# Two edits to a decoder kernel on one core: the last down stage's sums begin one gate pair later, and the gates' first product reads hi and lo token factors side by side

## The chip, the cores and the metric

The kernel runs as one program on one core of a Trainium2 chip. The metric is the device time of one execution in microseconds (us). The median of the runs shown is compared, 1024.15 us for the kernel before. A profiled execution is a run of its own, a little longer; its span goes from the first to the last instruction of the program.

The engines are named as in the profile: PE is TensorE (matmuls), PEld its weight loads, DVE is VectorE, ACT is ScalarE, POOL is GpSimd, SP is SyncE. SP issues most DMA transfers, POOL issues those that add while they copy.

## What is computed

A trunk of two layers on 512 tokens of width 1024, in float32. Layer 0 mixes tokens with a gated short convolution, layer 1 with sliding-window attention. Behind each stands a gated feed-forward block of inner width 2816, which takes most of the time:

```python
def swiglu(h, w_gate_up, w_down):
    g, u = jnp.split(h @ w_gate_up, 2, axis=-1)
    return (jax.nn.silu(g) * u) @ w_down

for l in range(DEPTH):
    h = h + rmsnorm(mixer(h), post_norm)          # short convolution, then attention
    ff = swiglu(rmsnorm(h, ffn_pre_norm[l]), ffn_w_gate_up[l], ffn_w_down[l])
    h = h + rmsnorm(ff, ffn_post_norm[l])
```

## The kernel before, in words

**Number format.** Each float32 factor is split into a high part (ACT copies it to the format fp32r) and a low part (DVE subtracts the high part from the whole). A product of two split factors is three matmuls: high by high, high by low, low by high. `mm3` (lines 190 to 193) issues them. For weights, `prepare` in `Job` makes the high part `whi` at line 469 and the low part `wlo` at line 470.

**Gates.** The 2816 inner columns are 22 slices of 128. Two are computed plainly (`project_first`); the other 20 are ten pairs, q = 0 to 9 in each layer, so 20 pairs in all. A pair multiplies a 2 by 2 arrangement of weight blocks by a 2 by 2 arrangement of token factors (left and right 256 tokens, upper and lower four of the eight token tiles) in seven products instead of eight. `gate_jobs` runs them in the order 1, 2, 6, 5, 7, 3, 4. Every product has eight steps: two outputs e, four tiles k of the contraction. Products 1, 6, 7 and 4 gather in a chain X of two PSUM banks, product 2 in a bank Y, products 5 and 3 in a bank Z.

The token factors of products 6, 5, 7 and 4 are sums of blocks that `factors` makes. They lie side by side, high part in columns 0 to 511 and low part in columns 512 to 1023 of one wide tile. So in chain X a step of products 6, 7 and 4 needs one matmul of `whi` with 512 columns (high and low of 256 tokens, line 1047) and one of `wlo` with 256 columns (line 1050). The left half of the bank then holds the products with the high part, the right half that of `whi` with the low part, and `take` adds both halves to what was gathered. Product 1 reads token tiles 0 to 3 as they are, whose high and low parts lie in separate tiles, and goes through `mm3`: three matmuls of 256 columns a step, all into the left half.

`take` (from line 998) follows each product: for products 1, 6 and 4 ACT copies the left half of a bank into `st` (line 1024), and, except for product 1, DVE adds the right half (line 1026, which the profile shows under line 1008, the helper that issues the addition). Product 7 has four such additions. Behind product 4 DVE multiplies gate and up parts (line 1029). Then come the sums and splits that the down stage needs (`pair_sums`), spread over the next jobs.

**Down stages.** The inner slices are worked off in five rounds (`ROUNDS`). Rounds 0 to 3 multiply by the down weights in seven products as well (`seven`), each round one pair behind its gates; round 4 closes the layer plainly (`close`, or the tail of the kernel). The order in a layer is: pairs 0, 1, 2, down 0, pairs 3, 4, down 1, pairs 5, 6, down 2, pairs 7, 8, 9, down 3. Down 3 is the last down stage.

**The line of jobs.** `in_line` runs these products as jobs. While job j is on PE, the weights of job j + 3 are split on ACT and DVE (`LINE_LEAD`), with four buffers each for `whi` and `wlo` (`N_W`). The raw weights come by SP's DMA (line 440 in `Raw.fetch`) into seven raw tiles (`N_RAW`): the next fetch is issued when a raw tile has been used up.

**Sums of weights.** The seven products need sums of weight blocks. Where a sum isn't made by DVE from raw tiles (line 457; pairs q = 1, 2, 3, 4, 5 and 7, the list `ADDED`), POOL makes it in HBM by DMA ahead of time. `Sums` has four steps: copies of blocks (four of them), two additions, one addition, one addition. `BEGIN` names the event at which each sum begins: `"0p5": "d03"` begins the sums of down stage 3 of layer 0 behind gate pair 5. Events in a layer are `p0` to `p9` (end of a pair) and `s0` to `s3` (end of a down stage). `sum_on` takes one step of every sum under way at each event, and `issue` (line 538) hands the transfers to POOL a few per job, each behind ACT's split of a coming job.

**Buffers.** Tiles come from pools: `big` has 43 slots of 512 columns (`N_SLOT`), `wides` 14 tiles of 1024 columns (`N_WIDE`). The split token factors are pairs of slots: `split` in `Update` (line 338) for the norms, line 645 for the convolution. So are the rotated queries and keys (`rope_split`, line 1245) and the attention outputs (`out` in `Heads`, line 1390). In attention the order of the work is written out by hand (`ORDER`).

Of the kernel before, what the change touches and what calls it, by code (L numbers as in the profile page):

```python
# [11 lines left out]
F32R = mybir.dt.float32r  # L12
# [6 lines left out]
S = 512  # L19
KT = D // P  # L20
# [7 lines left out]

BEGIN = {
# [4 lines left out]
}  # L34


# [15 lines left out]
    "L": "low", "W": "weigh", "O": "out", "Q": "project", "R": "rotate", "H": "split",  # L52
    "G": "weights", "Z": "project", "z": "out",
}
N_SLOT, N_WIDE, N_RAW, N_W = 43, 14, 7, 4
EARLY = 4
HD = 64
NH = 16
# [14 lines left out]
def yoco_kernel(  # L73
# [42 lines left out]
    def slot(s, dt=F32, w=S):  # L116
        return big.tile([P, w], dt, tag="slot", name=name(s), padded_shape=[P, S])

    def wide(s, dt=F32):
        return wides.tile([P, D], dt, tag="wide", name=name(s))  # L120
# [118 lines left out]
    class Update:  # L239
# [3 lines left out]
        def __init__(self, mix, gain, gpres):  # L243
            self.mix, self.gpres, self.gain = mix, gpres, gain
            self.s, self.v, self.r = (
                small.tile([P, n], F32, tag=tag, name=name(tag))
                for tag, n in (("us", 12), ("uv", 8), ("ur", 8))
            )
            self.x = [[None] * KT for _ in gpres]
            self.xn, self.banks, self.parts = {}, {}, {}  # L250
            self.leaves = False

        def load(self, queue=nc.sync):
# [82 lines left out]
                                        ident)  # L336

        def split(self, n, f, hf):
            if self.x[n][f] is None:
                self.x[n][f] = (slot("xhi", F32R), slot("xlo", F32R))  # L340
            hi, lo = self.x[n][f]
            c = slice(hf * 256, (hf + 1) * 256)
            src = self.banks[f % 4, hf][:, (f // 4) * 256 : (f // 4 + 1) * 256]
            nc.scalar.activation(hi[:, c], src, AF.Copy, scale=g(self.gpres[n], f))
            nc.vector.scalar_tensor_tensor(
                out=lo[:, c], in0=src, scalar=g(self.gpres[n], f), in1=hi[:, c].bitcast(F32),
                op0=ALU.mult, op1=ALU.subtract,
            )
# [15 lines left out]
        def factors(self):  # L364


            x = self.x[0]
            made = {p: [] for p in range(1, 8)}
            for p, k0, c in ((1, 0, 0), (2, 4, 0), (3, 4, 256)):
                made[p] = [[a[:, c : c + 256] for a in x[k0 + k]] for k in range(4)]  # L370
            for j in range(2):
                q11, q21, q12, q22 = (self.parts[i, hf, j] for hf in range(2) for i in range(2))

                nc.vector.tensor_tensor(out=q11, in0=q11, in1=q12, op=ALU.subtract)
                nc.vector.tensor_tensor(out=q12, in0=q22, in1=q12, op=ALU.subtract)
                nc.vector.scalar_tensor_tensor(out=q22, in0=q22, scalar=-1.0, in1=q11,
                                               op0=ALU.mult, op1=ALU.subtract)
                nc.vector.scalar_tensor_tensor(out=q21, in0=q22, scalar=-1.0, in1=q21,
                                               op0=ALU.mult, op1=ALU.subtract)
                for p, q in ((6, q22), (5, q11), (7, q12), (4, q21)):  # L380
                    two = wide("xt", F32R)
                    hi, lo = two[:, :S], two[:, S:]
                    two = two.rearrange("p (i c) -> p i c", i=2)
                    nc.scalar.activation(hi, q, AF.Copy)
                    nc.vector.tensor_tensor(out=lo, in0=q, in1=hi.bitcast(F32),
                                            op=ALU.subtract)
                    made[p] += [[hi[:, c : c + 256], lo[:, c : c + 256], two[:, :, c : c + 256]]
                                for c in (0, 256)]
            return made
# [252 lines left out]
        return product  # L642


    xs = [(slot("xhi", F32R), slot("xlo", F32R)) for _ in range(KT)]
    rows = slot("rrow")
    cols = small.tile([P, 4], F32, tag="cols", name=name("cols"))
    ws = [[wsp.tile([P, D], F32R, tag=tag, name=name(tag)) for tag in ("whi", "wlo")]
# [306 lines left out]
    def ffn(l, before, ahead, gain, gpres, following):  # L955

        xs = before.x[0]
# [18 lines left out]
        def gate_jobs(q, factors, out, to, then):  # L976
# [24 lines left out]
            def take(p):  # L1001
                x, y, z = (banks.get(c) for c in "XYZ")
                st, u, gr = kept
                g0, g1 = (gr.rearrange("p (e h c) -> p e h c", e=2, h=2)[:, :, h]
                          for h in range(2))

                def add(out, a, b):
                    nc.vector.tensor_tensor(out=out, in0=a, in1=b, op=ALU.add)  # L1008

                if p == 2:  # L1010
                    add(g0, tiles(y), tiles(st))
                elif p == 5:
                    nc.scalar.activation(u, z, AF.Copy)
                elif p == 3:
                    add(g1, tiles(z), tiles(st))
                else:
                    for e in range(2):
                        a, b = x[e][:, :256], x[e][:, 256:]
                        ste, ue = (v[:, e * 256 : (e + 1) * 256] for v in (st, u))
                        if p == 7:  # L1020
                            add(ue, a, ue)
                            add(ue, b, ue)
                            continue
                        nc.scalar.activation(ste, a, AF.Copy)  # L1024
                        if p != 1:
                            add(ste, b, ste)
                if p == 4:
                    for g, m in ((g0, st), (g1, u)):
                        nc.vector.scalar_tensor_tensor(out=g, in0=tiles(m), scalar=-1.0, in1=g,
                                                       op0=ALU.mult, op1=ALU.mult)  # L1030

            def run(p):
                def products(job):
                    if not kept:
                        kept.extend([slot("st"), slot("st"), wide("gr")])
                    whi, wlo = split[p] if p in split else job.w
                    c = chain[p]
                    opened = c not in banks
                    if opened:
                        banks[c] = ([bank("gx", pools[c]) for _ in range(2)] if c == "X"  # L1040
                                    else bank("g" + c.lower(), pools[c]))
                    steps = [(e, k, slice(e * S + k * P, e * S + (k + 1) * P))
                             for e in range(2) for k in range(4)]
                    kw = {"skip_group_check": True}
                    if c == "X" and len(factors[p][0]) == 3:
                        for e, k, kk in steps:
                            nc.tensor.matmul(banks[c][e], whi[:, kk], factors[p][k][2],  # L1047
                                             start=opened and k == 0, stop=False, **kw)
                        for e, k, kk in steps:
                            nc.tensor.matmul(banks[c][e][:, :256], wlo[:, kk], factors[p][k][0],  # L1050
                                             start=False, stop=k == 3 and p == 4, **kw)
                    else:
                        for e, k, kk in steps:
                            out = (banks[c][e][:, :256] if c == "X"
                                   else banks[c][:, e * 256 : (e + 1) * 256])
                            mm3(out, whi[:, kk], wlo[:, kk], *factors[p][k][:2],
                                opened and k == 0 and (c == "X" or e == 0),
                                e == 1 and k == 3 and p in (2, 3), **kw)
                    take(p)
                return products  # L1060
# [181 lines left out]
        eng.tensor_tensor(out=a, in0=a, in1=sh, op=ALU.add)  # L1242
        return a

    def rope_split(a, eng):
        hi, lo = slot("rhi", F32R), slot("rlo", F32R)
        nc.scalar.activation(hi, a, AF.Copy)
        eng.tensor_tensor(out=lo, in0=a, in1=hi.bitcast(F32), op=ALU.subtract)
        return hi, lo


    class Queries:
# [16 lines left out]
            self.rot = rope(self.ps, eng)  # L1269

        def split(self, eng=nc.gpsimd):
            self.hi, self.lo = rope_split(self.rot, eng)

    class Heads:

# [111 lines left out]
                    skip_group_check=True)  # L1387

        def out(self):
            hi, lo = slot("ohi", F32R), slot("olo", F32R)  # L1390
            nc.scalar.activation(hi, self.po, AF.Copy)
            nc.vector.tensor_tensor(out=lo, in0=self.po, in1=hi.bitcast(F32), op=ALU.subtract)
            at.append((hi, lo))
# [224 lines left out]
```

## Time and profile before

| what | us |
|---|---|
| median of 3 runs (1024.09 to 1025.18) | 1024.15 |
| the profiled execution | 1026.6 |
| its span | 1024.8 |
| PE busy | 1013.6 |
| DVE busy | 857.8 |
| ACT busy | 580.7 |

How to read it: the profile's busy time of PE is the time in which any matmul is under way. Matmuls overlap and their ends are modelled, so the distance between the starts of two matmuls says what one costs, and the duration does not. In a row of the timeline stand the start and the duration in us, the engine, the line of the code, the operation, what it writes and reads, its shape, and in brackets the idle time of the engine before it with what ended it. A row with x8 is eight instructions merged. The chain of waits starts from the last instruction and goes back at each step to what released it. DMA rows tell the time from issue to landing.

### The profile page before, as it was taken

The numbers are of one execution on the slowest core, as the hardware profiler recorded it, in microseconds if no ns is written. First come the engines' busy times: TensorE is split into PE (matmuls) and PEld (weight loads), VectorE is DVE, ScalarE is ACT, GpSimd is POOL, SyncE is SP. The second block draws the span as 40 slices with busy tenths as digits, with TensorE's granted clock in tenths as the row PEclk, the third lists the DMA queues.
The fourth block names the chain that finished last, engine by engine and source line by source line (L and its number), as shares of the span: only waits on it lengthen the run. The fifth ranks groups of instructions, "written<-read, shape, count | busy, mean of one in ns | idle before, by whom it ended". The sixth has DMA issues, their size and how long they took to land.

```text
span 1024.8 us, 16537 instructions
## 1 busy us (share of the span) xinstructions
PE 1013.6 (99%) x6168; PEld 901.8 (88%) x6168; DVE 857.8 (84%) x1440; ACT 580.7 (57%) x1035; POOL 196.7 (19%) x259
## 2 busy tenths in 40 slices
PE   9999999999999999999999999999999999999997
PEld 8888888999899898898898888889998998989986
DVE  5766768889789988988869998778997898889896
ACT  7222445875655454566476776667666554645641
POOL 0443033112111111000122653232111010100001
PEclk9999999999999999999999999999999999999999
DMA  9897789459979699778504889976899576998742
GB/s 356 287 255 232 187 254 348 140 169 281 344 249 299 195 302 318 256 215 303 182 1 152 199 234 281 246 260 156 262 289 333 169 247 228 299 294 245 242 150 82
DMA packets 66576, 244.52 MB, mean 239 GB/s; under 512 B 7872, under 2 KB 8384, under 8 KB 54720
## 3 DMA queue, kind: packets, MB, share of 16 engines
q1 hardware_dynamic: 51328, 145.98, 38.9%
q0 software_dynamic: 14592, 96.48, 37.2%
q8 instruction: 48, 0.79, 0.3%
q10 hardware_dynamic: 576, 1.02, 0.3%
q14 instruction: 32, 0.26, 0.1%
HBM read 237.15 MB, written 102.76 MB: 332 GB/s over the span
## 4 chain that ended last, share of the span: by engine, by line
PE 80%; DVE 11%; DMA 4%; ACT 2%; issue 2%; POOL 0%; DVEq 0%; ACTq 0%
PE gx L1047 10%; PE gx L1050 5%; DMA raw<-in_w_gb_dram 4%; PE pcub L193 4%; PE pcub L191 4%; PE pcub L192 4%; PE gz L193 3%; PE gz L192 3%; PE gz L191 3%; PE px L191 3%; PE px L192 3%; PE px L193 3%; PE pmix L192 2%; PE pmix L191 2%; PE pmix L193 2%
## 5 line engine op out<-in xcount | busy, mean ns | idle before, releaser
L470 DVE TENSOR_TENSOR wlo<-raw,whi 128x1024 fp32r<-128x1024 f32 x225 | 274.6, 1227 | 65.6 <-ACT whi L469 65.6
L469 ACT ACTIVATE whi<-raw 128x1024 fp32r<-128x1024 f32 x225 | 233.8, 1051 | 108.3 <-DVE raw L457 25.0
L1047 PE MATMUL gx<-xt,whi 128*128 128x512 f32 x480 | 120.4, 393 | 0.7 <-DVE st L1008 0.7
L1047 PEld LDWEIGHTS gx<-xt,whi 128*128 128x128 f32 x480 | 86.3, 189 | 16.6 <-DVE st L1008 1.2
L538 POOL DMA_DIRECT2D hsum<-in_w_gb_dram x96 | 63.4, 747 | 141.4 <-ACT whi L469 82.3
L1024 ACT ACTIVATE st<-gx 128x256 f32<-128x256 f32 x120 | 42.7, 379 | 60.8 <-PE gx L1050 36.4
L538 POOL DMA_DIRECT2D hsum<-hsum x32 | 25.2, 789 | 260.1 <-ACT whi L469 208.2
L1050 PEld LDWEIGHTS gx<-xt,wlo 128*128 128x128 f32 x480 | 65.5, 190 | 4.7
L1050 PE MATMUL gx<-xt,wlo 128*128 128x256 f32 x480 | 66.9, 282 | 0.0
L1008 DVE TENSOR_TENSOR st<-gx,st 128x256 f32<-128x256 f32 x160 | 62.8, 420 | 3.4 <-ACT st L1024 1.6
L192 PE MATMUL pcub<-xhi,whi 128*128 128x512 f32 x168 | 65.4, 389 | 0.0
L191 PE MATMUL pcub<-xlo,whi 128*128 128x512 f32 x168 | 65.4, 389 | 0.0
L193 PE MATMUL pcub<-xhi,wlo 128*128 128x512 f32 x168 | 65.4, 389 | 0.0
L1063 ACT ACTIVATE gr<-gr 128x1024 f32<-128x1024 f32 x20 | 21.3, 1063 | 50.6 <-DVE gr L1008 50.6
L191 PE MATMUL px<-wlo,ahi 128*128 128x512 f32 x120 | 46.8, 390 | 0.1
L192 PE MATMUL px<-whi,ahi 128*128 128x512 f32 x120 | 46.7, 389 | 0.0
L193 PE MATMUL px<-whi,alo 128*128 128x512 f32 x120 | 46.7, 389 | 0.0
L193 PE MATMUL gx<-xhi,wlo 128*128 128x256 f32 x160 | 45.4, 284 | 0.8 <-DVE wlo L470 0.8
L193 PE MATMUL gz<-xhi,wlo 128*128 128x256 f32 x160 | 45.5, 284 | 0.0
L191 PE MATMUL gx<-xlo,whi 128*128 128x256 f32 x160 | 45.4, 283 | 0.0
L191 PE MATMUL gy<-xlo,whi 128*128 128x256 f32 x160 | 45.3, 283 | 0.0
L192 PE MATMUL gy<-xhi,whi 128*128 128x256 f32 x160 | 45.3, 283 | 0.0
(265 smaller groups left out, 3062.8 us busy)
## 6 DMA issues: line engine op xcount, KB each, us to landing
hsum<-in_w_gb_dram POOLq DMA_DIRECT2D x96, 512.0 KB, 7.8
raw<-hsum SPq DMA_DIRECT2D x88, 512.0 KB, 7.9
raw<-in_w_gb_dram SPq DMA_DIRECT2D x60, 512.0 KB, 7.7
hsum<-in_w_dn_dram POOLq DMA_DIRECT2D x36, 512.0 KB, 9.1
raw<-in_w_dn_dram SPq DMA_DIRECT2D x32, 512.0 KB, 6.1
hsum<-hsum POOLq DMA_DIRECT2D x28, 512.0 KB, 6.7
raw<-in_w_in_dram SPq DMA_DIRECT2D x21, 512.0 KB, 8.1
hsum<-in_w_dn_dram POOLq DMA_DIRECT2D x12, 768.0 KB, 12.2
```

Source lines behind the costliest of these rows:

```text
L191: nc.tensor.matmul(out, whi, xlo, start=start, stop=False, **kw)
L192: nc.tensor.matmul(out, whi, xhi, start=False, stop=False, **kw)
L193: nc.tensor.matmul(out, wlo, xhi, start=False, stop=stop, **kw)
L469: self.begun = nc.scalar.activation(hi[:, :n], raw, AF.Copy)
L470: nc.vector.tensor_tensor(out=lo[:, :n], in0=raw, in1=hi[:, :n].bitcast(F32), op=ALU.subtract)
L538: nc.gpsimd.dma_start(dst, src, max_dma_last_dim=4 * 4 * S, **kw))
L1008: nc.vector.tensor_tensor(out=out, in0=a, in1=b, op=ALU.add)
L1024: nc.scalar.activation(ste, a, AF.Copy)
L1047: nc.tensor.matmul(banks[c][e], whi[:, kk], factors[p][k][2], start=opened and k == 0, stop=False, **kw)
L1050: nc.tensor.matmul(banks[c][e][:, :256], wlo[:, kk], factors[p][k][0], start=False, stop=k == 3 and p == 4, **kw)
L1063: nc.scalar.activation(kept[2], kept[2], AF.Silu)
```

## The change

It has three parts.

1. `BEGIN`: the sums of the last down stage of each layer (`d03`, `d13`) begin behind pair 6 instead of pair 5.
2. Token tiles 0 to 3 of the norm ahead of a feed-forward block are split into one wide tile, high and low side by side (`BOTH = 4`), and `factors` hands product 1, whose four tiles these are, the view of both parts. So product 1 takes the wide form in all 20 pairs: eight matmuls of 512 columns with `whi`, then eight of 256 columns with `wlo`, in place of 24 of 256 columns. Products 2, 3 and 5 stay as they are. `take` now adds the right half of the banks for product 1 too, two additions on DVE.
3. The pools change from 43 slots and 14 wide tiles to 35 and 18. Beside the token tiles, the convolution's first four, the rotated queries and the first four attention outputs move from slots to wide tiles.

```diff
-    "0f1": "g05", "0p0": "g06", "0p1": "d02", "0p2": "g07", "0p3": "g08", "0s1": "g09", "0p5": "d03",
+    "0f1": "g05", "0p0": "g06", "0p1": "d02", "0p2": "g07", "0p3": "g08", "0s1": "g09", "0p6": "d03",
...
-    "1f0": "g15", "1f1": "g16", "1p0": "d12", "1p2": "g17", "1p3": "g18", "1s1": "g19", "1p5": "d13",
+    "1f0": "g15", "1f1": "g16", "1p0": "d12", "1p2": "g17", "1p3": "g18", "1s1": "g19", "1p6": "d13",
...
-N_SLOT, N_WIDE, N_RAW, N_W = 43, 14, 7, 4
+N_SLOT, N_WIDE, N_RAW, N_W = 35, 18, 7, 4
+BOTH = 4
...
         def split(self, n, f, hf):
+            if self.x[n][f] is None and n == 0 and f < BOTH:
+                two = wide("xhl", F32R)
+                self.x[n][f] = two[:, :S], two[:, S:]
+                self.both[f] = two.rearrange("p (i c) -> p i c", i=2)
...
             for p, k0, c in ((1, 0, 0), (2, 4, 0), (3, 4, 256)):
-                made[p] = [[a[:, c : c + 256] for a in x[k0 + k]] for k in range(4)]
+                made[p] = [[a[:, c : c + 256] for a in x[k0 + k]]
+                           + [two[:, :, c : c + 256] for two in self.both[k0 + k :][:1] if two]
+                           for k in range(4)]
...
                         nc.scalar.activation(ste, a, AF.Copy)
-                        if p != 1:
-                            add(ste, b, ste)
+                        add(ste, b, ste)
...
-                    if c == "X" and len(factors[p][0]) == 3:
+                    if c == "X":
                         for e, k, kk in steps:
                             nc.tensor.matmul(banks[c][e], whi[:, kk], factors[p][k][2],
                                              start=opened and k == 0, stop=False, **kw)
...
-            out = (banks[c][e][:, :256] if c == "X"
-                   else banks[c][:, e * 256 : (e + 1) * 256])
...
-    def rope_split(a, eng):
-        hi, lo = slot("rhi", F32R), slot("rlo", F32R)
+    def rope_split(a, eng, large=False):
+        hi, lo = halves("rhl", F32R) if large else (slot("rhi", F32R), slot("rlo", F32R))
...
-            hi, lo = slot("ohi", F32R), slot("olo", F32R)
+            if self.t < BOTH:
+                hi, lo = halves("ohl", F32R)
+            else:
+                hi, lo = slot("ohi", F32R), slot("olo", F32R)
```

More of the change, by code (lines that the diff above doesn't have):

```diff
@@ L250, in __init__ @@
             self.xn, self.banks, self.parts = {}, {}, {}
+            self.both = [None] * KT
             self.leaves = False
@@ L642, in seven @@
         return product
-    xs = [(slot("xhi", F32R), slot("xlo", F32R)) for _ in range(KT)]
+    xs = [halves("xhl", F32R) if k < BOTH else (slot("xhi", F32R), slot("xlo", F32R))
+          for k in range(KT)]
     rows = slot("rrow")
@@ L1053, in products @@
                         for e, k, kk in steps:
-                            out = (banks[c][e][:, :256] if c == "X"
-                                   else banks[c][:, e * 256 : (e + 1) * 256])
-                            mm3(out, whi[:, kk], wlo[:, kk], *factors[p][k][:2],
-                                opened and k == 0 and (c == "X" or e == 0),
+                            mm3(banks[c][:, e * 256 : (e + 1) * 256], whi[:, kk], wlo[:, kk],
+                                *factors[p][k][:2], opened and e == k == 0,
                                 e == 1 and k == 3 and p in (2, 3), **kw)
@@ L1271, in split @@
         def split(self, eng=nc.gpsimd):
-            self.hi, self.lo = rope_split(self.rot, eng)
+            self.hi, self.lo = rope_split(self.rot, eng, True)
     class Heads:
```

## The prediction

> **What bounds the kernel now.** I read the page first, then the windows of the stages, then single stretches of the timeline. The profiled execution took 1026.6 us, 1.8 more than its span. Of the rows below, the first two are the page's busy times and its chain of waits; a window's columns are its length, the busy time of PE, PEld, DVE, ACT and POOL, the clock, the DMA share and GB/s.
>
> ```profile
> PE 1013.6 (99%) x6168; PEld 901.8 (88%) x6168; DVE 857.8 (84%) x1440; ACT 580.7 (57%) x1035; POOL 196.7 (19%) x259
> PE 80%; DVE 11%; DMA 4%; ACT 2%; issue 2%; POOL 0%; DVEq 0%; ACTq 0%
> ```
> ```profile
> 391.00:410.00 19.00, 19.00 (x86) 15.77 (x86) 14.68 (x21) 6.73 (x9) 2.36 (x3) 1.00 1.02 322
> 410.00:431.00 21.00, 19.97 (x139) 18.20 (x138) 20.29 (x30) 11.77 (x18) 1.56 (x2) 1.00 0.77 256
> ...
> 500.00:600.00 100.00, 98.75 (x662) 85.94 (x662) 86.24 (x226) 67.98 (x177) 41.03 (x49) 1.00 0.44 123
> 600.00:700.00 100.00, 99.57 (x646) 87.00 (x645) 82.71 (x215) 71.93 (x187) 34.65 (x41) 1.00 0.89 257
> ```
>
> The end is set by the stream of matmuls, at clock 1.00: time is won by a shorter stream or by closing its few holes. A matmul's duration is no price, since matmuls overlap; what counts is the distance between starts. These rows of PE's timeline run from product 4 of one gate pair to product 5 of the next (start, duration).
>
> ```profile
> 221.35 2.00 PE L1047 MATMUL gx<-xt,whi 128*128 128x512 f32 x8
> 223.19 1.11 PE L1050 MATMUL gx<-xt,wlo 128*128 128x256 f32 x8
> 224.15 0.28 PE L191 MATMUL gx<-xlo,whi 128*128 128x256 f32 x1
> 227.03 0.28 PE L191 MATMUL gy<-xlo,whi 128*128 128x256 f32 x1
> 229.91 2.00 PE L1047 MATMUL gx<-xt,whi 128*128 128x512 f32 x8
> 232.70 0.28 PE L191 MATMUL gz<-xt,whi 128*128 128x256 f32 x1
> ```
>
> In product 4 the 8 wide matmuls take 223.19 - 221.35 = 1.84 us (0.230 each) and the 8 narrow ones 224.15 - 223.19 = 0.96 (0.120 each). Product 1, 24 narrow ones, takes 227.03 - 224.15 = 2.88 us. Product 6, already in the wide form, takes 232.70 - 229.91 = 2.79.
>
> The largest hole lies in pair 7 of each layer. The next rows are the first matmul of product 1 of pairs 7, 8 and 9 in layer 0 (with the one that stalls), then of pairs 7 and 8 in layer 1.
>
> ```profile
> 410.35 0.39 PE L191 MATMUL gx<-xlo,whi 128*128 128x256 f32 x1
> 411.61 0.39 PE L193 MATMUL gx<-xhi,wlo 128*128 128x256 f32 x1 [0.76 <-DVE wlo L470]
> 431.91 0.28 PE L191 MATMUL gx<-xlo,whi 128*128 128x256 f32 x1
> 451.81 0.28 PE L191 MATMUL gx<-xlo,whi 128*128 128x256 f32 x1
> ...
> 915.65 0.28 PE L191 MATMUL gx<-xlo,whi 128*128 128x256 f32 x1
> 936.28 0.28 PE L191 MATMUL gx<-xlo,whi 128*128 128x256 f32 x1
> ```
>
> An undisturbed pair takes 451.81 - 431.91 = 19.90 us. Pair 7 takes 21.56 in layer 0 and 20.63 in layer 1, so 1.66 + 0.73 = 2.4 us are lost. The row names wlo as what was late; in the chain of waits stand the weight fetches behind it, 19 and 20 us under way:
>
> ```profile
> 389.06 20.07 DMA raw<-in_w_gb_dram
> 896.80 19.04 DMA raw<-in_w_gb_dram
> ```
>
> **The change part by part.** *The last down stage's sums, one pair later.* First POOL's issues from the end of pair 5 (371 us) on, in its timeline; then, for line 440, the least, median and greatest time to landing of the fetches issued in 351 to 371, 376 to 410 and 418 to 456 us.
>
> ```profile
> 376.00 0.80 POOL L538 DMA_DIRECT2D hsum<-hsum  x1 [9.17 <-ACT a L580]
> 376.52 1.89 POOL L538 DMA_DIRECT2D hsum<-in_w_gb_dram  x2
> 381.73 0.53 POOL L538 DMA_DIRECT2D hsum<-in_w_dn_dram  x1 [3.31 <-ACT whi L469]
> ...
> 387.69 0.50 POOL L538 DMA_DIRECT2D hsum<-in_w_dn_dram  x1 [0.97 <-ACT whi L469]
> 394.07 0.79 POOL L538 DMA_DIRECT2D hsum<-hsum  x1 [5.88 <-ACT whi L469]
> ...
> 436.61 0.78 POOL L538 DMA_DIRECT2D hsum<-hsum  x1 [16.60 <-ACT whi L469]
> ```
> ```profile
> DMA to landing us min/median/max: 5.8/7.9/8.6
> ...
> DMA to landing us min/median/max: 10.2/16.4/20.1
> ...
> DMA to landing us min/median/max: 3.3/4.8/8.7
> ```
>
> After pair 5 POOL issues seven transfers in 12 us: three for pairs 8 and 9, then the four copies from w_dn that this part moves. There the fetches go from 8 to 16 us. A fetch is issued seven raw tiles ahead, about 7 x 2.85 = 20 us, so one that takes 20 comes too late. With the change, the end of pair 5 issues three and the end of pair 6 (391 us) five: the four copies and the one of 394.07. Five is what stood behind 351 us (a sum of sums, four copies), where the fetches took 8 us and nothing stalled. All four steps move: the additions behind pair 6 go behind down stage 2, the next to behind pair 7, the last from 436.61 to behind pair 8, some 20 us later: about 456.5.
>
> SP must not fetch a sum before it is made. SP's rows of the tail, and the page's row for the slowest group of sums (KB each, median us to landing):
>
> ```profile
> 458.61 0.37 SPq L440 DMA_DIRECT2D raw<-hsum  x1
> ...
> 462.88 0.37 SPq L440 DMA_DIRECT2D raw<-hsum  x1
> ...
> 475.40 0.36 SPq L440 DMA_DIRECT2D raw<-hsum  x1
> ```
> ```profile
> hsum<-in_w_dn_dram POOLq DMA_DIRECT2D x12, 768.0 KB, 12.2
> ```
>
> The sum made last is fetched last, at 475.40; issued at 456.5, and even if it took the 12.2 us of the slowest group, it is there by 469. SP's queue, in which reloads of h stand behind that fetch, is not held. In POOL's queue nothing else stands between 400 and 480 us in this stage, so no one waits behind the moved transfers but the sums of pair 9, which go ahead of them. The other sums are a step earlier. So this part costs nothing there and gains between 0 and 2.4 us.
>
> I weigh a rule here. The Trainium skill, "DMA: Bandwidth & Descriptors", section "Queues, rings and completion order", says that each DMA engine takes turns between the queues that have work for it, a packet at a time. That speaks against the change: SP's fetches would share with POOL wherever the copies go. The trace agrees that they share (16.4 against 4.8 us), and by the rule alone the stall would move and this part would give nothing, which is rival B.
>
> *Product 1 in the wide form.* Tiles 0 to 3 are all that product 1 reads, so it changes in all 20 pairs; products 2, 3 and 5 stay narrow. By product 6 against product 1 it saves 2.88 - 2.79 = 0.09 us, 20 x 0.09 = 1.8 us. PE has 8 matmuls and 8 weight loads fewer per pair, and nothing is late in their place: product 2's weights are ready, as before every product of an undisturbed pair. The low weights are now wanted 1.84 us into the product and not at its third matmul, which would by itself hide the 0.76 us of 411.61.
>
> The Trainium skill, "TensorE: Matmul & The Clock Gate", section "Back-to-back issue gap", gives 518 cycles at 2.4 GHz for 512 columns and 262 for 256. A step would save 3 x 262 - 518 - 262 = 6 cycles, by an estimate from that page 0.4 us over 160 steps. The trace does not agree: its narrow matmuls stand 0.120 us apart, not 0.109. The rows decide for 1.8; that a wide one could cost as much as two narrow ones is rival C.
>
> *Two more additions on DVE per pair.* Product 1 now leaves a second half in its bank, which line 1026 adds, twice per pair: 40 additions. Rows of DVE around the same place, pair 2 of layer 0, and of its stage (204 to 475 us: busy, mean ns, idle before and what ended it):
>
> ```profile
> 245.88 0.75 DVE L1008 TENSOR_TENSOR st<-gx,st 128x256 f32<-128x256 f32 x2
> 246.67 1.29 DVE L1029 SCALAR_TENSOR_TENSOR gr<-st,gr 128x512 f32<-128x512 f32 x2
> 247.88 2.35 DVE L470 TENSOR_TENSOR wlo<-raw,whi 128x1024 fp32r<-128x1024 f32 x2
> ...
> 249.81 0.40 PE L1047 MATMUL gx<-xt,whi 128*128 128x512 f32 x1
> ...
> 257.26 1.23 DVE L470 TENSOR_TENSOR wlo<-raw,whi 128x1024 fp32r<-128x1024 f32 x1 [0.55 <-ACT whi L469]
> ```
> ```profile
> L470 DVE TENSOR_TENSOR wlo<-raw,whi 128x1024 fp32r<-128x1024 f32 x95 | 114.8, 1214 | 26.6 <-ACT whi L469 26.5
> ```
>
> Two additions are 0.75 us: 15 us on DVE, 7.5 per layer, and they are to lie in the 26.6 us that DVE waits in that stage for weights. They stand between the two splits of 247.88: the first, for product 6, ends about 249.1, the second, for product 5, would end at 251.0 and not 250.2. Product 5 starts 2.79 after 249.81, at 252.6, so 1.6 us are left. Queued behind are the split of a11, product 2's sum, product 7's split, each 0.75 later, until the gap of 0.55 at 257.26; 0.2 us stay over into the next pair, where product 6's split has 249.81 - 249.1 = 0.7 us to spare. That is the narrowest place, and only pairs 1 to 5 and 7, which also add raw weights (line 457), fill DVE so far. Product 6 must also wait until the additions have read its banks: the first ends at about 249.5, the second at 249.85, and the second bank is wanted 4 x 0.23 later. The ACT copies before them exist already. I take 0; the ends are 0 (work is only added) and 15 us. Were the cover gone, all 0.75 per pair would show.
>
> *Buffers.* Eight slots become four wide tiles; the token factors take just those in the convolution and feed-forward stages. In attention the rotated queries and four head outputs move instead. No row shows a buffer there that is waited for. The stage loses 1.25 + 0.43 us now (500 to 700 us); I take 0, with bounds of 1.7 either way.
>
> **The sum.** For the profiled execution 1026.6 - 1.8 - 2.4 = 1022.4 us. The median of the timed runs, 1024.15, is 2.45 below that execution; a part of the stall may be missing in them, between none and all. I take two thirds, 1.6 us: 1024.15 - 1.8 - 1.6 = 1020.8 us.
>
> **The rivals.**
> A, the forecast, both gains: 1020.8; by itself 1019.0 to 1022.1. Chance 0.62.
> B, the stall stays or moves to pair 7's fetches, since the bytes are the same: 1024.15 - 1.8 = 1022.4. For it speaks the share of 1.02 in 391 to 410 us; against it the five transfers behind 351 us. Chance 0.17.
> C, a wide matmul is worth two narrow ones: 1024.15 - 1.6 = 1022.6. Against it stands product 6. Chance 0.05.
> D, the other side: DVE sets the pace in the 12 pairs that add raw weights. If the gap of 0.55 can't be used, because ACT's split behind it waits too, each pays 0.75: 9.0, less 0.7 (8 other pairs at 0.09) and the 1.6 of the stall: 1030.9. It decides from where margin and gap, 0.7 + 0.55, fall below 0.75 + 0.09; they are above by 0.4. Chance 0.10.
> E, attention pays 1.7 for its fewer slots: 1022.5. Chance 0.06.
>
> **How the numbers follow.** A change of 0.2%, 2.05 us, is about what a measurement of this kernel can tell from none. Below 1022.1 lie A, less 0.02 at its edge, and 0.06 of B, C and E together, since each can come out 0.4 lower: faster 0.66. The rest of them, 0.24, is the same; D is slower, 0.10. The range goes from 1019.0 (all of the stall, and attention a little better) to 1024.0, which takes in B, C and E and leaves D and a small part of A below out.
>
> **What would show it.** Right: 160 PE instructions fewer; product 1 in 2.80 us and an undisturbed pair in 19.81; fetches issued in 376 to 410 us landing within 13 us; pair 7 as long as pair 8; L1008 on 128x256 x200, with PE's idle before products 5 and 6 near 0. Wrong: a wait for st or wlo in pairs 1 to 5 (D), a 20 us fetch behind pair 6 (B), product 1 still at 2.88 (C), new holes between 540 and 650 us (E).

## The result and the profile after

Over 21 runs each, the changed kernel has a median of 1023.26 us and the kernel before 1024.55 us: a ratio of 0.9987, with a 95% interval of 0.9981 to 0.9993. That is 1.3 us less, a gain that is clear of noise and smaller than 0.2%. The runs of before go from 1023.75 to 1026.30, those of the changed kernel from 1022.80 to 1023.78. The profiled execution of the changed kernel took 1023.55 us with a span of 1021.8, against 1026.6 and 1024.8 before: 3.0 us less in the profile, 1.3 in the medians. Three executions at a clock of 0.754 to 0.85 (1239.07, 1101.6 and 1099.83 us), where all others have 0.998 or 0.999, are left out of every median below.

In the code after the change, line 1055 is the wide matmul (1047 before), 1058 the narrow one (1050), 1017 the additions (1008), 478 the split of the low weights (470); the edits of the experiments shift these by a line or two.

First the page of the changed kernel, then PE's timeline around product 1 of pair 1.

```profile
PE 1011.7 (99%) x6008; PEld 893.5 (87%) x6008; DVE 869.4 (85%) x1480; ACT 582.3 (57%) x1035; POOL 197.3 (19%) x259
PE 90%; DVE 5%; ACT 2%; issue 1%; POOL 0%; DVEq 0%; ACTq 0%
```
```profile
221.49 2.00 PE L1055 MATMUL gx<-xt,whi 128*128 128x512 f32 x8
223.33 1.11 PE L1058 MATMUL gx<-xt,wlo 128*128 128x256 f32 x8
224.28 2.00 PE L1055 MATMUL gx<-xhl,whi 128*128 128x512 f32 x8
226.12 1.12 PE L1058 MATMUL gx<-xhl,wlo 128*128 128x256 f32 x8
227.07 0.28 PE L192 MATMUL gy<-xlo,whi 128*128 128x256 f32 x1
```

PE has 160 instructions fewer and DVE 40 more. DMA, 4% of the chain before, is gone from it. Product 1 takes 227.07 - 224.28 = 2.79 us, as product 4 does. Now the starts of pairs 7, 8 and 9 in layer 0 and of 7 and 8 in layer 1, POOL's issues from 381 to 404 us, and the time to landing of the fetches issued from 376 to 410 us, then of those from 376 to 391 and from 391 to 410 us alone.

```profile
409.94 0.39 PE L1055 MATMUL gx<-xhl,whi 128*128 128x512 f32 x1
429.73 0.40 PE L1055 MATMUL gx<-xhl,whi 128*128 128x512 f32 x1
449.54 0.40 PE L1055 MATMUL gx<-xhl,whi 128*128 128x512 f32 x1
...
913.59 0.39 PE L1055 MATMUL gx<-xhl,whi 128*128 128x512 f32 x1
933.37 0.40 PE L1055 MATMUL gx<-xhl,whi 128*128 128x512 f32 x1
```
```profile
381.35 0.78 POOL L546 DMA_DIRECT2D hsum<-in_w_gb_dram  x1 [3.62 <-ACT whi L477]
393.76 0.77 POOL L546 DMA_DIRECT2D hsum<-hsum  x1 [11.64 <-ACT whi L477]
395.23 0.53 POOL L546 DMA_DIRECT2D hsum<-in_w_dn_dram  x1 [0.69 <-ACT whi L477]
...
403.33 0.50 POOL L546 DMA_DIRECT2D hsum<-in_w_dn_dram  x1 [2.22 <-ACT whi L477]
```
```profile
DMA to landing us min/median/max: 5.3/7.6/13.0
...
DMA to landing us min/median/max: 6.3/10.1/13.0
...
DMA to landing us min/median/max: 5.3/7.5/7.8
```

The copies stand behind pair 6 now, the fetches land in 7.6 us at the median, not 16.4, and pair 7 takes 19.79 us, as pair 8 does (19.81). The slowest fetch, 13.0 us, was issued behind pair 5; behind pair 6, beside the five transfers, none took more than 7.8. Two places need a closer look: a wait in attention that the prediction took to be absent, and the narrow place in pair 2. The first rows below are DVE's, in attention and then in pair 2; the last is PE's product 6 in pair 2.

```profile
577.09 0.67 DVE L1246 TENSOR_TENSOR ra<-pk,ctab 128x512 f32<-128x512 f32 x1
579.02 0.69 DVE L1380 TENSOR_TENSOR plo<-pt,phi 128x512 fp32r<-128x512 f32 x1 [1.26 <-ACT se L1341]
...
248.04 1.22 DVE L478 TENSOR_TENSOR wlo<-raw,whi 128x1024 fp32r<-128x1024 f32 x1
249.18 0.75 DVE L1017 TENSOR_TENSOR st<-gx,st 128x256 f32<-128x256 f32 x2
249.84 1.22 DVE L478 TENSOR_TENSOR wlo<-raw,whi 128x1024 fp32r<-128x1024 f32 x1
```
```profile
249.76 0.62 PE L1055 MATMUL gx<-xt,whi 128*128 128x512 f32 x2
```

In attention DVE now stands for 1.26 us before it splits the probabilities `plo`. The row names ACT's last act before, which is not the cause: in the program this split waits for ACT alone before the change, and for PE as well after it, because the slot it is given is still read by PE. In pair 2 each of the two additions takes 0.42 us: the one that reads the first bank ends at 249.60, and product 6 begins to write that bank at 249.76; the second addition ends at 249.92, and product 6 comes to its bank only four wide matmuls later.

Since the first microseconds of a profile differ by several tenths from one execution to the next, I compare stages by their own length, from the starts on PE. From product 1 of pair 0 to the first matmul behind down 3, layer 0 took 270.64 us before and 268.06 after: the hole's 1.66 and 0.92 more. The same stretch of layer 1, up to the tail, took 269.59 and 268.04: 0.73 and 0.82. Attention (first scores to output projection) took 109.95 and 110.79. So in the profile the product gives 1.74, the hole 2.39, and attention takes 0.84 back; the 0.3 us by which this sum is above the 3.0 of the spans lie ahead of pair 0 (0.22 us later after the change) and in the tail.

### The profile page after: what moved, and what is told of

It reads as the page before. It is cut to its first block, busy times and chain, and to the rows that moved or that the text cites. A ratio compares the mean times of both kernels' runs of the same rounds, so it can differ in the third digit from the quotient of the medians.

```text
span 1021.8 us, 16273 instructions
## 1 busy us (share of the span) xinstructions
PE 1011.7 (99%) x6008; PEld 893.5 (87%) x6008; DVE 869.4 (85%) x1480; ACT 582.3 (57%) x1035; POOL 197.3 (19%) x259
## 4 chain that ended last, share of the span: by engine, by line
PE 90%; DVE 5%; ACT 2%; issue 1%; POOL 0%; DVEq 0%; ACTq 0%
PE gx L1055 14%; PE gx L1058 7%; PE pcub L193 4%; PE pcub L194 4%; PE pcub L192 4%; PE gz L194 4%; PE gz L192 4%; PE gz L193 4%; PE px L192 3%; PE px L193 3%; PE px L194 3%; PE pmix L193 2%; PE pmix L192 2%; PE pmix L194 2%; PE gy L193 2%; PE gy L192 2%
## 5 line engine op out<-in xcount | busy, mean ns | idle before, releaser
L1017 DVE TENSOR_TENSOR st<-gx,st 128x256 f32<-128x256 f32 x200 | 77.9, 419 | 2.6 <-ACT st L1033 0.5
L192 PE MATMUL gz<-xt,whi 128*128 128x256 f32 x160 | 45.3, 283 | 0.0
L193 PE MATMUL gz<-xt,whi 128*128 128x256 f32 x160 | 45.3, 283 | 0.0
L194 PE MATMUL gy<-xhi,wlo 128*128 128x256 f32 x160 | 45.3, 283 | 0.0
L192 PE MATMUL gz<-xlo,whi 128*128 128x256 f32 x160 | 45.3, 283 | 0.0
L194 PE MATMUL gz<-xt,wlo 128*128 128x256 f32 x160 | 45.3, 283 | 0.0
```

Source lines behind the costliest of these rows:

```text
L192: nc.tensor.matmul(out, whi, xlo, start=start, stop=False, **kw)
L193: nc.tensor.matmul(out, whi, xhi, start=False, stop=False, **kw)
L194: nc.tensor.matmul(out, wlo, xhi, start=False, stop=stop, **kw)
```

## The experiments

Theory: the three parts add, and what the prediction had wrong is sizes, because the timed runs have little of the hole and because the buffers cost something. Rivals: that the product or the additions are dearer than they look, and that attention's loss only follows from other times upstream. Kernels of one group below ran on the same chip, with medians of the kernel before of 1024.42, 1024.65 and 1024.53 us.

**First group.** The changed kernel once more.

> The changed kernel itself, once more, on the same chip as the three others. All theories: 1.0 to 1.7 us below the kernel before, its runs within 1.2 us of each other, an undisturbed pair of gates 19.81 us, pair 7 the same.

Measured: 1023.07 us (1022.82 to 1023.52), ratio 0.9987 (0.9978 to 0.9997), 1.35 below.

The later sums alone, on the kernel before:

```diff
-"0p5": "d03"    "1p5": "d13"
+"0p6": "d03"    "1p6": "d13"
```

> The kernel before with the later sums alone (down 3 behind pair 6). Theory: the hole of pair 7 goes away in both layers (pair 7 takes 19.90 us), but most timed runs of the kernel before have little of it, so the median falls by 0.2 to 0.8 us only, and the runs lie within 1.2 us where those of the kernel before spread over 2.5. The prediction's sizing: the median falls by 1.6 us. Rival B: pair 7 still loses 0.5 us or more and the median stays.

Measured: 1023.87 us (1023.40 to 1024.40), ratio 0.9994 (0.9985 to 1.0002), 0.55 below, with the runs within 1.0 us. Pairs 7 and 8 of both layers in its profile:

```profile
409.92 0.28 PE L191 MATMUL gx<-xlo,whi 128*128 128x256 f32 x1
429.81 0.28 PE L191 MATMUL gx<-xlo,whi 128*128 128x256 f32 x1
...
913.57 0.28 PE L191 MATMUL gx<-xlo,whi 128*128 128x256 f32 x1
933.46 0.28 PE L191 MATMUL gx<-xlo,whi 128*128 128x256 f32 x1
```

Pair 7 takes 19.89 us in both. The hole is closed, as the theory has it, and its share in the timed runs is about 0.55 us, with an interval that includes none. In the profile the two gate stages take 268.84 and 268.87 us, so there the hole was 1.80 and 0.72, and the wide product makes the rest of the way to 268.06 and 268.04: 1.6 us. Rival B falls.

The buffers alone, on the kernel before:

```diff
-N_SLOT, N_WIDE, N_RAW, N_W = 43, 14, 7, 4
+N_SLOT, N_WIDE, N_RAW, N_W = 35, 18, 7, 4
+# and the moves of the diff; product 1 stays narrow, the sums stay early
```

> The kernel before with the buffers of the changed one alone: 35 slots, 18 wide tiles, the same tiles moved; product 1 narrow, the sums early. Theory: attention loses 0.8 us, with DVE waiting about 1.2 us before the third split of head pair 0's probabilities, because that slot is still read by PE; median 0.5 to 1.0 us above the kernel before, all of it between 560 and 600 us. Rival: the 0.8 us is an effect of the shorter gate stage or of the moved sums on what runs beside attention; then this kernel equals the kernel before within 0.3.

Measured: 1025.17 us (1024.57 to 1026.84), ratio 1.0010 (1.0001 to 1.0018), 0.75 above. DVE's row, then from PE's timeline the first and the last matmul of attention:

```profile
579.99 0.69 DVE L1381 TENSOR_TENSOR plo<-pt,phi 128x512 fp32r<-128x512 f32 x1 [1.26 <-ACT se L1342]
```
```profile
549.99 0.38 PE L1307 MATMUL psc<-rlo,rhl 64*128 64x256 f32 x2
660.73 0.40 PE L192 MATMUL pmix<-wlo,ohi 128*128 128x512 f32 x1
```

Attention takes 110.74 us, with the same wait of 1.26, without the product or the moved sums. The loss belongs to the buffers.

The changed kernel with one edit in attention:

```diff
-                phi, plo = slot("phi", F32R), slot("plo", F32R)
+                phi, plo = (halves("phl", F32R) if self.t < 3
+                            else (slot("phi", F32R), slot("plo", F32R)))
```

> The changed kernel with one edit: the split probabilities of the first three head pairs lie in wide tiles, which are free then, instead of slots. Theory: DVE no longer waits for PE there, and the median is 0.6 to 1.0 us below the changed kernel, about 2.1 below the kernel before. Rival: the wait was only the last of several that end together, and the kernel equals the changed one within 0.3.

Measured: 1022.85 us (1022.40 to 1023.30), 0.22 below the changed kernel on the same chip. The expectation of 0.6 to 1.0 missed; its rival, equal within 0.3, fits.

**Second group.** The same kernel, for its profile (one execution, 1022.49 us): DVE at the split of the probabilities, then the first and the last matmul of attention on PE.

> The same kernel as the run with the split probabilities in wide tiles, for a profile at full clock. Theory, corrected by that run's 0.2 us: the wait of DVE for that slot is gone, but another buffer's wait stands a little later in the same two iterations and keeps 0.4 to 0.7 of the 0.8 us. Rival: attention is as long as in the kernel before (109.95 us from the first scores to the output projection) and the lack lies elsewhere.

```profile
576.28 0.67 DVE L1246 TENSOR_TENSOR ra<-pk,ctab 128x512 f32<-128x512 f32 x1
576.87 0.68 DVE L1381 TENSOR_TENSOR phl<-pt,phl 128x512 fp32r<-128x512 f32 x1
```
```profile
548.32 0.39 PE L1306 MATMUL psc<-rlo,rhl 64*128 64x256 f32 x2
658.29 0.40 PE L192 MATMUL pmix<-wlo,ohi 128*128 128x512 f32 x1
```

DVE goes on without a wait and attention takes 109.97 us, as before the change. No second wait took its place in attention; the corrected theory, too, was wrong. In the profile the whole 0.8 of attention is back. The tail, from its first matmul to the end of the span, takes 45.79 us against 45.62 in the control of the first group, so some of it is lost again there.

The changed kernel without the additions of product 1:

```diff
-                        add(ste, b, ste)
+                        if p != 1:
+                            add(ste, b, ste)
```

> The changed kernel without the 40 additions of product 1 (the contribution of the low token parts to that product's own term is left out). Theory: they are covered, so the time is that of the changed kernel within 0.3 us (1022.8 to 1023.5) and a pair takes 19.81 us in both. Rival D: DVE sets the pace in part, and this kernel is 0.7 us or more below the changed one.

Measured: 1023.19 us (1022.74 to 1023.86), the changed kernel's time; pair 1 starts 19.81 us after pair 0 in both. In the medians the 15 us of additions cost nothing. In the profile they cost 0.1 us in each layer: product 7 of pair 2 takes 2.90 us with them and 2.80 without, and the gate stages 268.06 and 268.04 against 267.95 and 267.95.

The additions issued twice:

```diff
                         add(ste, b, ste)
+                        if p == 1:
+                            add(ue, b, ste)
```

> The changed kernel with the two additions of product 1 issued twice (the second pair writes into a buffer that is overwritten later). It asks how far the cover reaches. By the prediction's reckoning 1.25 us of margin and gap stand against 0.84 a pair; with twice the additions it is 1.6, so in the 12 pairs that add raw weights up to 0.3 us each would show, 1 to 4 us in all, first in pairs 1 and 2 and before products 6 and 5. Rival: the cover is wider than that and the time is that of the changed kernel within 0.5 us.

Measured: 1027.68 us (1027.56 to 1028.40), 4.6 above the changed kernel (1023.07 on this chip), more than the expected 1 to 4. The cover ends close behind the present additions.

The changed kernel with the sums early:

> The changed kernel with the sums of down 3 behind pair 5 as before. Theory: the product gains 1.6 and the buffers cost 0.8, and the hole of pair 7 is back in some executions: median 1023.3 to 1023.8, spread 1.5 us or more. The low weights are wanted later in product 1, so of the hole the part before product 1's third matmul is gone. Rival: with DVE's 0.75 us more in pair 7 the hole is deeper than before and the median is at or above that of the kernel before.

Measured: 1025.29 us (1023.65 to 1026.52), 0.64 above the kernel before, ratio 1.0005 (0.9996 to 1.0014). Three runs lie at 1023.65 to 1023.78, the others at 1025.0 or more. The rival holds: the median is at that of the kernel before or above it. Product 6 of pair 7 in both layers, and DVE's rows ahead of the second:

```profile
415.99 0.73 PE L1055 MATMUL gx<-xt,whi 128*128 128x512 f32 x2 [0.34 <-DVE st L1017]
...
920.94 0.73 PE L1055 MATMUL gx<-xt,whi 128*128 128x512 f32 x2 [0.93 <-DVE st L1017]
```
```profile
915.75 1.23 DVE L478 TENSOR_TENSOR wlo<-raw,whi 128x1024 fp32r<-128x1024 f32 x1 [2.90 <-ACT whi L477]
916.89 1.22 DVE L465 TENSOR_TENSOR raw<-raw,raw 128x1024 f32<-128x1024 f32 x1
918.03 1.28 DVE L647 TENSOR_TENSOR mix<-mix,px 128x512 f32<-128x512 f32 x2
919.32 1.23 DVE L478 TENSOR_TENSOR wlo<-raw,whi 128x1024 fp32r<-128x1024 f32 x1
920.47 0.75 DVE L1017 TENSOR_TENSOR st<-gx,st 128x256 f32<-128x256 f32 x2
```

Late weights hold DVE for 2.90 us; what was due meanwhile follows without a break, and the additions come last. Product 6 writes the banks that they read, so it waits for them, although its own low weights are ready at 920.55 and it wants them only 1.84 us after its start.

**Third group.** The control, and the edit in attention again.

> The changed kernel as a control on the same chip. All theories: 1022.8 to 1023.6 us, 1.0 to 1.7 below the kernel before.

> The split probabilities of three head pairs in wide tiles, timed again beside the changed kernel. In the profile at full clock the 0.8 us of attention were back in full, while the first timing gave 0.2. Theory: 0.4 to 0.9 us below the control. Rival: in executions without a profile DVE has another cover there and the two agree within 0.2.

Measured: 1023.19 us (1022.75 to 1023.66) and 1022.89 (1022.29 to 1023.64), 0.30 less. The second profile of the edit has no wait either. Twice the gain came out at 0.2 to 0.3 us in the medians and 0.8 in the profile's attention, so it misses the expected 0.4 again. With 10 or 11 runs that overlap on each side, 0.2 to 0.3 us can't be told from none. The tail of this profile, 45.76 us, is 0.16 longer than the control's again; why the rest doesn't arrive in the medians stays open.

One more addition per pair, three instead of two:

```diff
                         add(ste, b, ste)
+                        if p == 1 and e == 0:
+                            add(ue, b, ste)
```

> The changed kernel with one more addition per pair (three instead of two, 0.37 us more on DVE). Twice as many additions cost 4.5 us. Theory of an edge (cover of about 0.4 us a pair beyond the two): nothing to 1.0 us more than the control. Rival: the cost grows evenly with the additions, then 2 us or more.

Measured: 1026.21 us (1025.73 to 1026.62), 3.0 above the control, against the 0 to 1.0 of the theory. Product 6 in pairs 1 and 2 of layer 0, then DVE's rows in pair 2, then the sum of such waits of PE (us in total, times, longest) in this run and in the one with four additions:

```profile
229.83 0.47 PE L1057 MATMUL gx<-xt,whi 128*128 128x512 f32 x1 [0.17 <-DVE st L1017]
250.21 0.70 PE L1057 MATMUL gx<-xt,whi 128*128 128x512 f32 x2 [0.27 <-DVE st L1017]
```
```profile
248.05 1.22 DVE L478 TENSOR_TENSOR wlo<-raw,whi 128x1024 fp32r<-128x1024 f32 x1
249.19 1.21 DVE L1017 TENSOR_TENSOR st<-gx,st 128x256 f32<-128x256 f32 x3
250.31 1.22 DVE L478 TENSOR_TENSOR wlo<-raw,whi 128x1024 fp32r<-128x1024 f32 x1
```
```profile
PE gx L1057 <- DVE st L1017: 1.3, 6, 0.3
...
PE gx L1057 <- DVE st L1017: 2.3, 10, 0.3
```

Again product 6 waits for the additions, not for its weights: its start moves to 0.55 us after product 2's last matmul (249.66), where 0.12 is due. An edge there is, but it lies at the present two additions and not 0.4 us beyond them. The added one reads the first bank again, the bank that product 6 writes first. Only pairs 1, 2 and 9 of each layer wait, six in all, and start 0.3 to 0.4 us later than in the control (the idle time in the rows counts from the modelled end of the matmul before); the other 14 pairs pay next to nothing, pairs 3, 4, 5 and 7 among them, which add raw weights. With four additions product 7 of pairs 1 and 2 waits as well, ten waits in all. So the two additions cost nothing in the medians, the third 3.0 us in all and the fourth 1.6. The rival's 2 us or more is met, its even growth is not.

The changed kernel with the sums early and without the additions:

> The changed kernel with the sums of down 3 behind pair 5 as before, and without the additions of product 1 (the contribution of the low token parts to that product's own term is left out). With the additions this was 1025.4 us. Theory: what made the hole of pair 7 deeper was that product 6 waits for the additions, which stand behind late weights in DVE's queue; without them the median falls to 1023.0 to 1024.2. Rival: the additions are not the cause (the wide product is earlier at late weights, or the buffers), and it stays above 1024.8.

Measured: 1023.75 us (1023.12 to 1025.48), ratio 0.9995 (0.9986 to 1.0004), 1.54 below the same kernel with the additions. PE's waits for DVE's additions, with the additions of product 1 and then without:

```profile
PE gx L1055 <- DVE st L1017: 1.3, 2, 0.9
...
PE gx L1056 <- DVE st L1017: 0.4, 1, 0.4
```

The theory holds: the additions are what made the hole deeper. The one wait that is left stands at product 7 of pair 7 in layer 1, for the additions behind product 6. Without the additions of product 1 the early sums cost 1023.75 - 1023.19 = 0.56 us, as on the kernel before.

## Why the prediction was right in its direction and wrong in its sizes

It gave 1020.8 us and a range of 1019.0 to 1024.0; the median is 1023.26, inside. The direction came, the gain is 1.3 instead of the 3.35 forecast, and it lies in what the prediction called the same. That the median lies inside is owed to the width of the range, drawn to take in B, C and E: two terms were off by 1.05 and 0.75 us, both to the same side, and of these rivals only E came true, in part.

*Product 1: right.* 0.09 us a pair by the rows, 1.8 in all. The stages show 1.74, or 1.6 against the kernel with the later sums alone, and 1.8 without the additions (the two stages take 537.71 us with the later sums alone and 535.90 in the run without the additions). No timed run has the product and the later sums without the smaller pools; in the medians 1.35 - 0.55 + 0.75 = 1.55 is left to it if those three add. The Trainium skill's cycles ("TensorE: Matmul & The Clock Gate", "Back-to-back issue gap", given there for a matmul by itself) would have given 0.4; the trace decided rightly, and rival C fell.

*The hole: mechanism right as far as it went, size wrong.* It went, in every profile with the later sums. The step that failed is "I take two thirds, 1.6 us": the runs had 0.55. The number came from one profiled execution, 1026.6 us, slower than any of the 21 timed runs of before (1026.30 at most, median 1024.55), and the hole differed even between its two layers. The only stall that the prediction shows is that of product 1 for late weights. The profile before has a second one, of product 7 of pair 7, first in layer 0, then in layer 1:

```profile
423.33 0.50 PE L1047 MATMUL gx<-xt,whi 128*128 128x512 f32 x1 [0.28 <-DVE st L1008]
...
927.71 0.50 PE L1047 MATMUL gx<-xt,whi 128*128 128x512 f32 x1 [0.47 <-DVE st L1008]
```

It waits for the additions behind product 6, which read its banks and come late in DVE's queue. That is about a third of the hole in layer 0 and all of it in layer 1, and it is the same wait that the additions behind product 1 later ran into. The Trainium skill's rule of the queues ("DMA: Bandwidth & Descriptors", "Queues, rings and completion order") agrees with the trace in that fetches are slower the more transfers run beside them (16.4 us at the median beside seven transfers in 12 us, 4.8 where POOL issues three in some 40 us); no run shows the turns themselves. That the stall would move by it did not come: behind pair 6 the fetches took 7.8 us at most, as the prediction read it from the five transfers behind 351 us, and the 13.0 us of the slowest one behind pair 5 are less than the 20 that seven raw tiles cover. Rival B fell.

*The buffers: wrong.* "No row shows a buffer there that is waited for. I take 0." The row could not show it, since the old pools had room. The runs showed 0.8 us in the profile, where moving the split probabilities gave it back, and 0.75 in the medians (between 0.1 and 1.8 by the interval of the ratio), where moving them gave 0.2 to 0.3; how much of the 0.75 is this wait stays open. Rival E named the place and bounded it at 1.7. With 0.55 and 0.75 in place of 1.6 and 0, the sum is 1024.15 - 1.8 - 0.55 + 0.75 = 1022.55; the runs shown then had 1024.15, the later ones 0.4 more, which leaves 0.3 us of the 1023.26 unexplained.

*The additions: right that they are covered, wrong about the slack.* In the changed kernel they cost nothing in the medians and 0.2 us in the profile. The prediction saw both ends, product 5's weights (1.6 us to spare) and product 6's banks, and even worked out that the first bank is free at about 249.5, with product 6 at 249.81; but rival D's point of decision counted the weights' margin and the gap, and left out these 0.3 us, the least of all. By the rows it was 0.16 us (249.60 to 249.76), and where product 6 does wait it starts 0.05 to 0.15 us behind the end of the addition, so at most 0.1 us was left. A cost of D's kind was one third of a microsecond of DVE time away, and it fell on pairs 1, 2 and 9, not on the 12 pairs that add raw weights.

*That the parts add: wrong, and nowhere stated.* On the kernel before the later sums give 0.55 us. On the kernel with the wide product they give 1025.29 - 1023.07 = 2.2, because without them late weights run into the additions. The product with its buffers alone is no gain that the runs show.

The kernel with the split probabilities moved has the lowest medians, 1022.85 and 1022.89 us, 1.6 below the kernel before in both timings; its 0.2 to 0.3 us to the changed kernel are within the spread of the runs.

## What to carry to other kernels

Work that is put on an engine beside the bottleneck is free only up to the first thing that waits for it: look for every waiter, and for buffers that are read as well as for results that are wanted, and take the smallest slack. A hole that hangs on transfers being just in time differs from run to run, so size it from the spread of many runs and not from one profile, the more so when that run is slower than the timed ones. When a pool gets smaller, count what is alive at the fullest point; a profile of the larger pool can't show the wait.

## What the runs showed that was not expected

Two changes that look independent, a DMA moved by 20 us and a matmul form, depend on each other: the first is worth 0.55 us alone and 2.2 us with the second. And a third of a microsecond of DVE work per pair, 7.5 us in all, took 3.0 us of the whole, in six pairs out of twenty, while the 15 us before it took nothing in the medians.
